# The product with w2 as seven products of quarters instead of eight, in 24 of its 32 row tiles

## The chip, the cores and the metric

The kernel runs on one core of a Trainium2 chip, as one program in one launch. The metric is the device time in microseconds; for a pair of kernels it is measured on the same chip. The kernel before took 1195.74 us, the median of three runs between 1192.88 and 1196.31.

## The reference

The reference is a decoder trunk of two layers on 512 tokens of 1024 columns, all in float32. Each layer is a token mixer and an MLP, and each of the four parts ends in a layer norm:

```python
D_MODEL = 1024; SEQ = 512; DEPTH = 2; D_FF = 4 * D_MODEL
ALPHA = (2 * DEPTH) ** 0.25
x = layer_norm(ALPHA * x + mixer(x), g, b)             # stick-breaking attention and SSM, then sparse attention
x = layer_norm(ALPHA * x + square(relu(x @ w1)) @ w2, g, b)     # w1: 1024 x 4096, w2: 4096 x 1024
```

Only the MLP is changed. Let H stand for the squared relu, 512 tokens by 4096.

## The kernel before

A float32 product is made of three products on TensorE in a format that it reads at one column per cycle. Each operand is split into a high part (a cast to that format, on ScalarE, line 104, tile `whi`) and a low part (the operand less its high part, on VectorE, line 105, tile `wlo`, for some tiles on GpSimd instead). Then high by high, high by low and low by high are added up in one accumulator. The activations are kept transposed, as `xhi` and `xlo`.

The MLP (function `mlp`) goes through the 4096 columns of H in eight groups of 512. For each group it computes four row tiles of H, 128 rows by 512 tokens each: a tile is 24 matmuls of 128x512 (lines 131 to 133; eight slices of the 1024 model columns, three matmuls each) into an accumulator `psa`. ScalarE takes the relu (line 222) and writes its square as the high part (line 224); VectorE squares the relu too (line 223) and subtracts the high part from it (line 225). Then the group's 512 rows of w2 are multiplied in: for each half of the columns and each of four token tiles, 12 matmuls of 128x512 (`mlp_block`, lines 255 to 257) into an accumulator `psb`, which VectorE adds to `x` (line 262). A group thus has 96 matmuls with w1 and 96 with w2. An MLP has 768 and 768.

The first four tiles of each MLP are computed in two halves of the tokens (`proj_halves`), so that they can begin as soon as two token tiles have left the layer norm ahead of it. For each token tile the layer norm (`layer_norm`) is a chain on VectorE: two statistics (line 181), their sum (182), the variance (183), a power on GpSimd (184), two scalings (185, 189), then TensorE transposes the tile (line 199), ScalarE casts the transpose (202) and VectorE subtracts (203). The out projection of the mixer, whose blocks (lines 716 to 718 and the addition to `x` on line 721 or 723) feed the layer norm, runs interleaved with it.

The order of the instructions on each engine is set when the kernel is built, by a scheduler that works from the program's order, the dependences and the free buffers; at run time each engine takes its instructions in that order and waits where an operand is not there. `raw` has three buffers, `whi` and `wlo` four each in each of two pools, `psb` four. Weights are loaded by DMAs that SyncE issues in its own fixed order.

Of the kernel before, what the change touches and what calls it, by code (L numbers as in the profile page):

```python
# [8 lines left out]
F32 = mybir.dt.float32  # L9
F32R = mybir.dt.float32r  # L10
AF = mybir.ActivationFunctionType
ALU = mybir.AluOpType
# [3 lines left out]
P = 128  # L16
S = 512
D = 1024
KT = D // P
NB = S // P  # L20
FF = 4096
ALPHA = 4.0 ** 0.25
# [13 lines left out]
class Trunk:  # L36
# [50 lines left out]
        self.n += 1  # L87
        return f"{s}_{self.n}"

    def w_tiles(self, pool=None):  # L90
        wp = pool or self.wp
        return (wp.tile([P, 1024], F32, tag="raw", bufs=3, name=self.nm("raw")),
                wp.tile([P, 1024], F32R, tag="whi", bufs=4, name=self.nm("whi")),
                wp.tile([P, 1024], F32R, tag="wlo", bufs=4, name=self.nm("wlo")))

    def weights(self, srcs, n=1024, eng=None, pool=None, parts=1):

        nc = self.nc
        raw, hi, lo = self.w_tiles(pool)
# [8 lines left out]
    def w_cols(self, w, c0, eng=None, pool=None):  # L108
# [4 lines left out]
        hi, lo = self.weights(srcs, eng=eng, pool=pool)  # L113
        return hi.rearrange("p (k c) -> p k c", c=P), lo.rearrange("p (k c) -> p k c", c=P)

    def w_rows(self, w, r0, c0, eng=None, pool=None, parts=1):
# [9 lines left out]
        hi, lo = self.weights(srcs, eng=eng, pool=pool, parts=parts)  # L126
        return hi.rearrange("p (k c) -> p k c", c=512), lo.rearrange("p (k c) -> p k c", c=512)

    def mm3(self, ps, lhi, llo, rhi, rlo, start, stop):
# [73 lines left out]
            nc.vector.tensor_tensor(self.xlo[:, 4 * h:4 * h + 4, tok], pv, hi.bitcast(F32), ALU.subtract)  # L203

    def mlp(self, w1, w2, g, b, last):
        nc = self.nc
        if self.n_mlp == 0:
            self.open_psb()
            self.kept = False
        self.n_mlp += 1  # L210
        with self.tc.tile_pool(name=self.nm("mlp"), bufs=2, side="right", reuse_waits="tile") as hp:
            ng = FF // 512
            for grp in range(ng):
                hhi = hp.tile([P, 4, S], F32R, tag="hhi", name=self.nm("hhi"))
                hlo = hp.tile([P, 4, S], F32R, tag="hlo", name=self.nm("hlo"))
                if grp == 0:
                    pss = self.proj_halves([self.w_cols(w1, f * P, nc.gpsimd, hp) for f in range(4)])
# [8 lines left out]
                ws = [[self.w_rows(w2, grp * 512 + i * 256, half * 512, pool=hp if half or grp < ng - 1 else self.wp)  # L226
                       for i in range(2)] for half in range(2)]
                part = lambda half, h=(hhi, hlo), ws=ws: (*h, ws[half])
                if grp < ng - 2:
                    for half in range(2):  # L230
                        for t in range(NB):
                            self.mlp_block([part(half)], t, half, grp == 0)
                elif grp == ng - 2:
                    for t in range(NB):
                        self.mlp_block([part(0)], t, 0, False)
                    held = part(1)
                else:
                    def both(t):
                        self.mlp_block([part(0)], t, 0, False)
                        n = 256 if last and t == NB - 1 else 512  # L240
                        for c0 in range(0, 512, n):
                            self.mlp_block([held, part(1)], t, 1, False, c0, n)
                    self.blocks_and_norms([lambda t=t: both(t) for t in range(NB)], self.ln_params(g, b), last,
                                          2 if last else 1)

    def mlp_block(self, parts, t, half, first, c0=0, n=512):
# [830 lines left out]
```

## Time and profile before

| what | value |
|---|---|
| median of three runs | 1195.74 us |
| the profiled execution | 1195.17 us, of it 1193.4 us in the span |
| TensorE busy | 1141.6 us, 96% of the span |
| VectorE, ScalarE, GpSimd busy | 61%, 37%, 16% |
| granted clock of TensorE, mean | 0.987 of full speed |

A full clock (1.00) is the level of 2.4 GHz, 0.50 the level of 1.2 GHz. The span has four stages: the first mixer until about 265 us, the first MLP until 600, the second mixer until 860, the second MLP from there to the end. Matmuls are pipelined in the profile: each lasts longer than the time to the next one, so the cost of a row of matmuls is read from their starts, and the time that a row lasts tells when its result can be used. The chain that ended last is followed back from the last instruction; what stands in it set the end.

### The profile page before, as it was taken

Reading aid. Unit: us, or ns where it says so; the run is one execution under the profiler, and the core shown is the slowest. Engines: PE = TensorE matmul, PEld = TensorE weight load, DVE = VectorE, ACT = ScalarE, POOL = GpSimd, SP = SyncE. Lnnn points to the kernel's source line nnn. Section 1 sums busy time; section 2 is a strip of 40 time slices with the busy share of each in tenths; the row PEclk is TensorE's granted clock in tenths of the full one; section 3 lists DMA queues with packets and bytes.
Section 4 is the critical chain, followed back from the end, with each engine's and each line's share of the span. In section 5 each row is a group of like instructions: output and inputs, shape, how many; then the busy total and the mean of one; then the engine's idle time right before and its main releaser. Section 6 shows DMA issues by size and latency. Waiting matters only on the chain.

```text
span 1193.4 us, 15777 instructions
## 1 busy us (share of the span) xinstructions
PE 1141.6 (96%) x6004; PEld 952.2 (80%) x6004; DVE 724.5 (61%) x1183; ACT 443.2 (37%) x734; POOL 193.2 (16%) x209
## 2 busy tenths in 40 slices
PE   7989998999999999999999959998999999999997
PEld 6878776798888888888898847777988888888886
DVE  7996598685444444444568997539544444444436
ACT  5534487323322332323145437643322332332320
POOL 1044130450000000000021735327000000000001
PEclk9998999999999999999999979999999999999999
DMA  7536772643332332332155840025422332332201
GB/s 239 141 79 147 196 228 54 177 120 111 106 98 79 106 107 71 106 96 51 36 146 150 216 136 1 2 60 172 140 89 88 106 106 71 106 106 74 69 1 71
DMA packets 147307, 127.00 MB, mean 106 GB/s; under 512 B 24352, under 2 KB 115296, under 8 KB 147232
## 3 DMA queue, kind: packets, MB, share of 16 engines
q1 hardware_dynamic: 145552, 123.59, 36.2%
q10 hardware_dynamic: 1680, 2.41, 0.6%
q8 instruction: 47, 0.77, 0.3%
q14 instruction: 28, 0.23, 0.1%
HBM read 105.80 MB, written 5.37 MB: 93 GB/s over the span
## 4 chain that ended last, share of the span: by engine, by line
PE 82%; DVE 11%; DMA 3%; issue 2%; ACT 1%; SPq 1%; POOLq 0%; DVEq 0%; POOL 0%; ACTq 0%
PE psa L132 11%; PE psa L133 11%; PE psa L131 11%; PE psb L257 10%; PE psb L256 10%; PE psb L255 10%; PE pso L824 3%; PE pst L817 2%; DVE acc L989 2%; DVE top L988 2%; PE psl L1011 2%; PE psb L716 2%; PE psb L718 2%; PE psb L717 2%; DVE sh L498 1%
## 5 line engine op out<-in xcount | busy, mean ns | idle before, releaser
L104 ACT CAST whi<-raw 128x1024 fp32r<-128x1024 f32 (+1 forms) x177 | 184.5, 1048 | 482.3 <-PE psb L257 249.5
L105 DVE TENSOR_TENSOR wlo<-raw,whi 128x1024 fp32r<-128x1024 f32 (+1 forms) x142 | 179.8, 1268 | 194.3 <-ACT whi L104 194.0
L132 PE MATMUL psa<-xlo,whi 128*128 128x512 f32 (+1 forms) x720 | 267.1, 372 | 2.4 <-DVE xlo L203 2.4
L133 PE MATMUL psa<-xhi,wlo 128*128 128x512 f32 (+1 forms) x720 | 267.6, 372 | 0.0
L131 PE MATMUL psa<-xhi,whi 128*128 128x512 f32 (+1 forms) x720 | 265.9, 372 | 0.2 <-ACT xhi L202 0.2
L255 PE MATMUL psb<-whi,hhi 128*128 128x512 f32 (+1 forms) x520 | 200.6, 386 | 0.0
L256 PE MATMUL psb<-wlo,hhi 128*128 128x512 f32 (+1 forms) x520 | 200.5, 386 | 0.0
L257 PE MATMUL psb<-whi,hlo 128*128 128x512 f32 (+1 forms) x520 | 193.0, 386 | 0.0
L262 DVE TENSOR_TENSOR x<-x,psb 128x512 f32<-128x512 f32 (+1 forms) x105 | 69.2, 679 | 148.3 <-PE psb L257 148.2
L132 PEld LDWEIGHTS psa<-xlo,whi 128*128 128x128 f32 x720 | 136.4, 189 | 25.7 <-DVE xlo L203 2.6
L133 PEld LDWEIGHTS psa<-xhi,wlo 128*128 128x128 f32 x720 | 136.3, 189 | 23.0
L131 PEld LDWEIGHTS psa<-xhi,whi 128*128 128x128 f32 x720 | 135.7, 190 | 23.2 <-ACT xhi L202 0.5
L105 POOL TENSOR_TENSOR wlo<-raw,whi 128x1024 fp32r<-128x1024 f32 x35 | 93.6, 2686 | 144.8 <-ACT whi L104 143.7
L257 PEld LDWEIGHTS psb<-whi,hlo 128*128 128x128 f32 x520 | 97.7, 188 | 19.6
L256 PEld LDWEIGHTS psb<-wlo,hhi 128*128 128x128 f32 x520 | 97.7, 188 | 19.6
L255 PEld LDWEIGHTS psb<-whi,hhi 128*128 128x128 f32 x520 | 97.7, 188 | 19.5
L184 POOL TENSOR_TENSOR rs<-rs,two 128x1 f32<-128x1 f32 x16 | 21.1, 1318 | 408.8 <-DVE rs L183 408.7
L716 PE MATMUL psb<-whi,xhi 128*128 128x512 f32 x128 | 50.6, 400 | 2.3 <-DVE x L721 2.3
L717 PE MATMUL psb<-wlo,xhi 128*128 128x512 f32 x128 | 50.1, 392 | 0.8 <-DVE wlo L105 0.8
L718 PE MATMUL psb<-whi,xlo 128*128 128x512 f32 x128 | 50.4, 394 | 0.0
L225 DVE TENSOR_TENSOR hlo<-h,hhi 128x512 fp32r<-128x512 f32 x64 | 44.3, 693 | 6.4
L223 DVE TENSOR_TENSOR h<-r 128x512 f32<-128x512 f32 x64 | 43.8, 685 | 6.5 <-ACT r L222 6.5
(240 smaller groups left out, 1481.6 us busy)
## 6 DMA issues: line engine op xcount, KB each, us to landing
raw<-in_w_dram SPq DMA_DIRECT2D x128, 512.0 KB, 4.1
raw<-in_w_in_dram SPq DMA_DIRECT2D x29, 512.0 KB, 4.3
raw<-in_w_out_dram SPq DMA_DIRECT2D x16, 512.0 KB, 4.5
qst<-hl SPq DMA_DIRECT2D x48, 128.0 KB, 2.9
kst<-hl SPq DMA_DIRECT2D x24, 256.0 KB, 4.4
gb<-in_ln_g_dram SPq DMA_DIRECT2D x4, 512.0 KB, 3.7
gb<-in_ln_b_dram SPq DMA_DIRECT2D x4, 512.0 KB, 5.5
x<-in_x_dram SPq DMA_DIRECT2D x4, 512.0 KB, 6.8
```

Of the source, the lines that this page charges most:

```text
L104: nc.scalar.copy(hi[:, c], raw[:, c])
L105: (eng or nc.vector).tensor_tensor(lo[:, c], raw[:, c], hi[:, c].bitcast(F32), ALU.subtract)
L131: mm(ps, lhi, rhi, start=start, stop=False)
L132: mm(ps, lhi, rlo, start=False, stop=False)
L133: mm(ps, llo, rhi, start=False, stop=stop)
L255: nc.tensor.matmul(ps, lh, whi, start=f + i == 0, stop=False)
L256: nc.tensor.matmul(ps, lh, wlo, start=False, stop=False)
L257: nc.tensor.matmul(ps, ll, whi, start=False, stop=f == 3 and i == len(parts) - 1)
L262: nc.vector.tensor_tensor(xs, xs, ps, ALU.add)
L716: nc.tensor.matmul(ps, chi[:, k, tok], whi, start=i == 0, stop=False)
L717: nc.tensor.matmul(ps, chi[:, k, tok], wlo, start=False, stop=False)
L718: nc.tensor.matmul(ps, clo[:, k, tok], whi, start=False, stop=k == tiles[-1])
```

## The change

In each MLP the first six groups are taken in three chunks of 1024 rows, and the product of H with these rows of w2 is computed by Strassen's method in Winograd's form. The tokens, the 1024 rows and the columns are each cut in two, so that H gives four quarters (`a11`, `a21`: the first 512 rows, for tokens 0 to 255 and 256 to 511; `a12`, `a22`: the other 512 rows) and w2 four (`b11`, `b12`, `b21`, `b22`). Seven products of a combination of quarters with another take the place of eight. A product (lines 311 to 313) is 24 matmuls of 128x512 into two accumulators, so a chunk has 168 matmuls with w2 where two groups had 192. The combinations of quarters of w2 (line 293) and of H (lines 334, 345, 347, 354) and the additions of the accumulators to `x` (lines 320, 323) and to a buffer `u` (line 331) are VectorE's, except that ScalarE writes `u` the first time (line 329). `u` is added to three quarters of `x` at the end of the third chunk (line 367).

The tiles of H of a chunk stay float32: ScalarE takes the relu (line 227) and squares it in place (line 228). High and low parts are made of each combination just before its product (lines 298 and 299). The program writes one product, then one tile of H of the next chunk, and so on; after the seventh product come the last two tiles, and then the next chunk. The last two groups are computed as before (ScalarE now does the square and the cast, lines 237 and 238). GpSimd no longer subtracts for the four tiles after the first four of each MLP; VectorE does.

The other functions of the diff only pass a buffer's name on, so that the new tiles share space. Lines of the new kernel behind this place are 124 higher than before (the out projection's 716 to 723 are 840 to 847).

```diff
     def mlp(self, w1, w2, g, b, last):
...
-                for f in range(4):
-                    ps = pss[f] if grp == 0 else self.proj_fm(w1, grp * 512 + f * P, nc.gpsimd if grp == 1 else None)
-                    r = hp.tile([P, S], F32, tag="r", name=self.nm("r"))
-                    h = hp.tile([P, S], F32, tag="h", name=self.nm("h"))
-                    nc.scalar.activation(r, ps, AF.Relu)
-                    nc.vector.tensor_tensor(h, r, r, ALU.mult)
-                    nc.scalar.activation(hhi[:, f, :], r, AF.Square)
-                    nc.vector.tensor_tensor(hlo[:, f, :], h, hhi[:, f, :].bitcast(F32), ALU.subtract)
...
+            def up_raw(c, first=False):
+                hs = [h_tile(F32) for _ in range(2)]
+                pss = self.proj_halves([self.w_cols(w1, f * P, nc.gpsimd, hp, ("b21", "b22")[f // 2])
+                                        for f in range(4)]) if first else ()
+                for f in range(8):
+                    if f < len(pss):
+                        ps = pss[f]
+                    else:
+                        ps = self.proj_fm(w1, (c * 8 + f) * P, None)
+                    h = hs[f // 4][:, f % 4, :]
+                    nc.scalar.activation(h, ps, AF.Relu)
+                    nc.scalar.activation(h, h, AF.Square)
+                    yield hs
...
+            for hs in up_raw(0, True):
+                pass
+            u = hp.tile([P, 2, 512], F32, tag="u", bufs=1, name=self.nm("u"))
+            touched = set()
+            for c in range(3):
+                ups = up_raw(c + 1) if c < 2 else itertools.chain(up_split(6), up_split(7))
+                got = []
+                for _ in self.down_chunk(hp, w2, c * 1024, hs, u, touched, c == 2):
+                    got += itertools.islice(ups, 1)
+                got += ups
+                hs = got[-1]
...
+    def down_chunk(self, hp, w2, r0, hs, u, touched, last):
+        nc, mm = self.nc, self.nc.tensor.matmul
+        vec, act = nc.vector, nc.scalar
+        a11, a21 = hs[0][:, :, 0:256], hs[0][:, :, 256:512]
+        a12, a22 = hs[1][:, :, 0:256], hs[1][:, :, 256:512]
...
+        def halves(src, pool, c):
...
+            act.copy(hi, src)
+            vec.tensor_tensor(lo, src, hi.bitcast(F32), ALU.subtract)
+            return hi, lo
+
+        def product(a, b):
+            pss = [self.psb.tile([P, 512], F32, tag="psb", name=self.nm("psb")) for _ in range(2)]
+            ahi, alo = halves(a, self.wp, 256)
+            for i in range(2):
+                bhi, blo = halves(b[i], hp, 512)
+                for t, ps in enumerate(pss):
+                    tok = slice(t * P, (t + 1) * P)
+                    for k in range(2):
+                        lh, ll = ahi[:, 2 * i + k, tok], alo[:, 2 * i + k, tok]
+                        mm(ps, lh, bhi[:, k, :], start=i + k == 0, stop=False)
+                        mm(ps, lh, blo[:, k, :], start=False, stop=False)
+                        mm(ps, ll, bhi[:, k, :], start=False, stop=i + k == 2)
+            return pss
...
+        b12, b11 = load("b12", 0, 1), load("b11", 0, 0)
+        vec.tensor_tensor(a21, a21, a22, ALU.add)
+        combine(b12, b12, b11, ALU.subtract)
+        ps = product(a21, b12)
+        add(ps, 1, 1)
+        add(ps, 0, 1)
+        yield
+        b22 = load("b22", 1, 1)
+        ps = product(a11, b11)
+        add(ps, 0, 0)
+        gather(ps)
+        yield
+        vec.tensor_tensor(a11, a21, a11, ALU.subtract)
+        s4 = hp.tile([P, 4, 256], F32, tag="s4", bufs=1, name=self.nm("s4"))
+        vec.tensor_tensor(s4, a12, a11, ALU.subtract)
+        add(product(s4, b22), 0, 1)
+        yield
...
+        add(product(a22, b22), 1, 0, ALU.subtract)
+        if last:
+            for row, col in ((0, 1), (1, 0), (1, 1)):
+                xs = self.x[:, 2 * row:2 * row + 2, col * 512:col * 512 + 512]
+                vec.tensor_tensor(xs, xs, u, ALU.add)
+        yield
```

The scheduler's order is shown at three places. The first is TensorE in the first MLP, where the work with w1 ends and that with w2 begins. Before, behind the last tile of the second group (`psa_506`), stand blocks of its product (`psb_521`, `psb_522`), whose first operands are slices 0 to 2 of H (`hhi_483`):

```order
L132 MATMUL psa_506_2955<-xlo_72,whi_504_2950 128x512
L133 MATMUL psa_506_2955<-xhi_71,wlo_505_2951 128x512
L255 MATMUL psb_521_3010<-whi_510_2987,hhi_483_2836 128x512 [waits DVE_49,Activation_49]
L256 MATMUL psb_521_3010<-wlo_511_2988,hhi_483_2836 128x512
L257 MATMUL psb_521_3010<-whi_510_2987,hlo_484_2837 128x512 [waits DVE_49]
L255 MATMUL psb_521_3010<-whi_510_2987,hhi_483_2836 128x512 [waits Activation_49]
```

Now, at the second chunk, behind the last of its eight tiles (`psa_570`) stands the first product (`psb_575`, `psb_576`), whose `whi_577` is the high part of `a21` plus `a22`:

```order
L132 MATMUL psa_570_3371<-xlo_72,whi_568_3366 128x512
L133 MATMUL psa_570_3371<-xhi_71,wlo_569_3367 128x512
L311 MATMUL psb_575_3409<-whi_579_3415,whi_577_3411 128x512 [waits Activation_49]
L312 MATMUL psb_575_3409<-wlo_580_3416,whi_577_3411 128x512
L311 MATMUL psb_576_3410<-whi_579_3415,whi_577_3411 128x512
L312 MATMUL psb_576_3410<-wlo_580_3416,whi_577_3411 128x512
L131 MATMUL psa_588_3459<-xhi_71,whi_586_3454 128x512 [waits Activation_49]
L132 MATMUL psa_588_3459<-xlo_72,whi_586_3454 128x512
L313 MATMUL psb_575_3409<-whi_579_3415,wlo_578_3412 128x512 [waits DVE_49]
```

The product that needs all eight tiles has moved to the place right behind the last of them. The second place is VectorE in the layer norm ahead of the first MLP. Before (`psb_393` to `psb_399` are blocks of the out projection, 723 is the addition to `x`):

```order
L723 TENSOR_TENSOR x_1307<-x_1307,psb_393_2234 128x512 [waits PE_49]
L181 BN_STATS st_404_2318<-x_1307 128x6 [waits DVE_49]
L723 TENSOR_TENSOR x_1307<-x_1307,psb_395_2248 128x512 [waits PE_49]
L181 BN_STATS st_404_2318<-x_1307 128x6 [waits DVE_49]
L182 BN_AGGR mv_405_2319<-st_404_2318 128x2 [waits DVE_49]
L183 TENSOR_SCALAR rs_406_2320<-mv_405_2319 128x1 [waits DVE_49]
L185 SCALAR_TENSOR_TENSOR x_1307<-x_1307,mv_405_2319,gb_169_1311 128x1024
```

Now the first combination of quarters of w2 (`b12` less `b11`, two tiles) stands among them:

```order
L847 TENSOR_TENSOR x_1307<-x_1307,psb_393_2234 128x512 [waits PE_49]
L181 BN_STATS st_404_2318<-x_1307 128x6 [waits DVE_49]
L847 TENSOR_TENSOR x_1307<-x_1307,psb_395_2248 128x512 [waits PE_49]
L181 BN_STATS st_404_2318<-x_1307 128x6 [waits DVE_49]
L293 TENSOR_TENSOR b12_472_2817<-b12_472_2817,b11_474_2821 128x1024 [waits DMAHW6_49,DMAHW4_49]
L182 BN_AGGR mv_405_2319<-st_404_2318 128x2 [waits DVE_49]
L293 TENSOR_TENSOR b12_473_2819<-b12_473_2819,b11_475_2823 128x1024 [waits DMAHW7_49,DMAHW5_49]
L847 TENSOR_TENSOR x_1307<-x_1307,psb_397_2262 128x512 [waits PE_49]
L183 TENSOR_SCALAR rs_406_2320<-mv_405_2319 128x1 [waits DVE_49]
L185 SCALAR_TENSOR_TENSOR x_1307<-x_1307,mv_405_2319,gb_169_1311 128x1024
```

Two subtractions came between the statistics and the scaling of the first token tile. The third place is TensorE ahead of the second MLP, behind the last block of the out projection (`psb_1279`, token tile 3). Before, the transposes of token tile 1 stand there (`pst_1284`, `pst_1286`), and then the first tiles of H (`psa_1316` to `psa_1319`):

```order
L718 MATMUL psb_1279_7190<-whi_1263_7083,xlo_72 128x512
L199 MATMUL pst_1284_7226<-ident_73,x_1307 128x128 [waits DVE_49]
L199 MATMUL pst_1284_7226<-ident_73,x_1307 128x128 x3
L199 MATMUL pst_1286_7233<-ident_73,x_1307 128x128 [waits PE_49]
L199 MATMUL pst_1286_7233<-ident_73,x_1307 128x128 x3
L131 MATMUL psa_1316_7320<-xhi_71,whi_1305_7297 128x256 [waits Activation_49]
```

Now those of token tile 2 stand there too (`pst_1305`, `pst_1307`):

```order
L842 MATMUL psb_1293_7213<-whi_1277_7106,xlo_72 128x512
L199 MATMUL pst_1298_7249<-ident_73,x_1307 128x128 [waits DVE_49]
L199 MATMUL pst_1298_7249<-ident_73,x_1307 128x128 x3
L199 MATMUL pst_1300_7256<-ident_73,x_1307 128x128 [waits DVE_49]
L199 MATMUL pst_1300_7256<-ident_73,x_1307 128x128 x3
L199 MATMUL pst_1305_7273<-ident_73,x_1307 128x128 [waits DVE_49,PE_49]
L199 MATMUL pst_1305_7273<-ident_73,x_1307 128x128 x3
L131 MATMUL psa_1330_7343<-xhi_71,whi_1319_7320 128x256 [waits Activation_49]
```

The first tile of H now stands behind the layer norm of a third token tile.

## Rows read from the trace of the kernel before

**Rows 1.** Busy time by stage: stretch, length, engines (instructions), clock, DMA share, GB/s.
```profile
265.00:600.00 335.00, 335.00 (x1535) 279.67 (x1534) 161.29 (x203) 100.12 (x129) 4.33 (x4) 1.00 0.30 89
860.00:1193.40 333.40, 325.77 (x1460) 270.53 (x1458) 156.97 (x199) 87.75 (x111) 5.83 (x4) 0.99 0.27 82
```
**Rows 2.** The page, part 5: groups, busy, mean ns, idle before and releaser.
```profile
L132 PE MATMUL psa<-xlo,whi 128*128 128x512 f32 (+1 forms) x720 | 267.1, 372 | 2.4 <-DVE xlo L203 2.4
L257 PE MATMUL psb<-whi,hlo 128*128 128x512 f32 (+1 forms) x520 | 193.0, 386 | 0.0
```
**Rows 3.** Timeline of TensorE in the first MLP: start, us, what.
```profile
320.24 0.39 PE L133 MATMUL psa<-xhi,wlo 128*128 128x512 f32 x1
...
328.17 0.39 PE L256 MATMUL psb<-wlo,hhi 128*128 128x512 f32 x1
```
**Rows 4.** Timelines of ScalarE and VectorE there.
```profile
320.48 1.05 ACT L104 CAST whi<-raw 128x1024 fp32r<-128x1024 f32 x1 [3.23 <-PE psa L132]
321.44 0.59 ACT L222 ACTIVATE r<-psa 128x512 f32<-128x512 f32 x1
322.06 0.63 ACT L224 ACTIVATE hhi<-r 128x512 fp32r<-128x512 f32 x1
...
321.56 1.23 DVE L105 TENSOR_TENSOR wlo<-raw,whi 128x1024 fp32r<-128x1024 f32 x1 [2.82 <-ACT whi L104]
329.05 1.29 DVE L262 TENSOR_TENSOR x<-x,psb 128x512 f32<-128x512 f32 x2 [4.86 <-PE psb L257]
```
**Rows 5.** Timeline of VectorE in the layer norm ahead of the first MLP.
```profile
235.70 2.42 DVE L185 SCALAR_TENSOR_TENSOR x<-x,mv,gb 128x1024 f32<-128x1024 f32 x1
...
242.18 1.27 DVE L185 SCALAR_TENSOR_TENSOR x<-x,mv,gb 128x1024 f32<-128x1024 f32 x1
243.37 0.68 DVE L723 TENSOR_TENSOR x<-x,psb 128x512 f32<-128x512 f32 x1
243.97 1.28 DVE L189 SCALAR_TENSOR_TENSOR x<-x,rs,gb 128x1024 f32<-128x1024 f32 x1
```
**Rows 6.** Timelines of GpSimd and TensorE there.
```profile
225.60 11.44 POOL L105 TENSOR_TENSOR wlo<-raw,whi 128x1024 fp32r<-128x1024 f32 x4 [21.72 <-ACT whi L104]
...
241.90 1.03 PE L199 MATMUL pst<-ident,x 128*128 128x128 f32 x8
245.53 0.60 PE L199 MATMUL pst<-ident,x 128*128 128x128 f32 x4
245.91 0.49 PE L716 MATMUL psb<-whi,xhi 128*128 128x512 f32 x1
```
**Rows 7.** Timeline of VectorE in the layer norm ahead of the second MLP.
```profile
811.26 2.22 DVE L105 TENSOR_TENSOR wlo<-raw,whi 128x1024 fp32r<-128x1024 f32 x1
828.41 3.32 DVE L185 SCALAR_TENSOR_TENSOR x<-x,mv,gb 128x1024 f32<-128x1024 f32 x1
```
**Rows 8.** Timeline of TensorE there, and at an earlier wait.
```profile
821.33 1.03 PE L199 MATMUL pst<-ident,x 128*128 128x128 f32 x8
829.81 0.74 PE L131 MATMUL psa<-xhi,whi 128*128 128x256 f32 x4 [0.24 <-ACT xhi L202]
832.98 0.38 PE L132 MATMUL psa<-xlo,whi 128*128 128x256 f32 x1 [2.43 <-DVE xlo L203]
...
229.84 0.47 PE L716 MATMUL psb<-whi,xhi 128*128 128x512 f32 x1 [2.05 <-DVE x L721]
```
**Rows 9.** Busy time and granted clock (third number from the end) around three waits.
```profile
230.00:231.00 1.00, 1.00 (x5) 0.82 (x5) 1.00 (x1) 0.00 (x0) 1.00 (x1) 1.00 1.02 303
834.00:835.00 1.00, 1.00 (x6) 1.00 (x6) 0.93 (x4) 0.00 (x0) 1.00 (x2) 0.50 0.04 10
836.00:837.00 1.00, 1.00 (x7) 1.00 (x6) 1.00 (x1) 0.00 (x0) 1.00 (x2) 0.50 1.09 329
714.00:715.00 1.00, 0.54 (x2) 0.54 (x3) 1.00 (x5) 0.56 (x2) 0.00 (x0) 0.50 0.00 0
716.00:717.00 1.00, 1.00 (x5) 0.91 (x4) 1.00 (x5) 0.99 (x5) 0.00 (x0) 0.50 0.00 0
```

More of the change, by code (lines that the diff above doesn't have):

```diff
@@ L88, in nm, with w_tiles, weights @@
         return f"{s}_{self.n}"
-    def w_tiles(self, pool=None):
+    def w_tiles(self, pool=None, tag=None):
         wp = pool or self.wp
-        return (wp.tile([P, 1024], F32, tag="raw", bufs=3, name=self.nm("raw")),
+        return (wp.tile([P, 1024], F32, tag=tag or "raw", bufs=2 if tag else 3, name=self.nm("raw")),
                 wp.tile([P, 1024], F32R, tag="whi", bufs=4, name=self.nm("whi")),
                 wp.tile([P, 1024], F32R, tag="wlo", bufs=4, name=self.nm("wlo")))
-    def weights(self, srcs, n=1024, eng=None, pool=None, parts=1):
+    def weights(self, srcs, n=1024, eng=None, pool=None, parts=1, tag=None):
         nc = self.nc
-        raw, hi, lo = self.w_tiles(pool)
+        raw, hi, lo = self.w_tiles(pool, tag)
         for view, src in srcs(raw):
@@ L106, in weights, with w_cols @@
         return hi, lo
-    def w_cols(self, w, c0, eng=None, pool=None):
+    def w_cols(self, w, c0, eng=None, pool=None, tag=None):
         def srcs(raw):
@@ L112, in srcs, with w_rows @@
                    w[:, c0:c0 + P].rearrange("(k p) c -> p k c", p=P))
-        hi, lo = self.weights(srcs, eng=eng, pool=pool)
+        hi, lo = self.weights(srcs, eng=eng, pool=pool, tag=tag)
         return hi.rearrange("p (k c) -> p k c", c=P), lo.rearrange("p (k c) -> p k c", c=P)
-    def w_rows(self, w, r0, c0, eng=None, pool=None, parts=1):
+    def w_rows(self, w, r0, c0, eng=None, pool=None, parts=1, tag=None):
         def srcs(raw):
@@ L125, in srcs @@
                     yield rv[:, k, :], wv[:, k, :]
[L126 removed]
+        hi, lo = self.weights(srcs, eng=eng, pool=pool, parts=parts, tag=tag)
         return hi.rearrange("p (k c) -> p k c", c=512), lo.rearrange("p (k c) -> p k c", c=512)
@@ new lines, in mlp @@
+            h_tile = lambda dt: hp.tile([P, 4, S], dt, tag="h", bufs=4, name=self.nm("h"))
+            def up_raw(c, first=False):
[11 more added lines that the diff above has]
+                    yield hs
@@ new lines, in up_split @@
+            def up_split(grp):
+                hhi, hlo = h_tile(F32R), h_tile(F32R)
+                for f in range(4):
+                    ps = self.proj_fm(w1, grp * 512 + f * P, None)
+                    h = hp.tile([P, S], F32, tag="r", bufs=1, name=self.nm("r"))
+                    nc.scalar.activation(h, ps, AF.Relu)
+                    nc.scalar.activation(h, h, AF.Square)
+                    nc.scalar.copy(hhi[:, f, :], h)
+                    nc.vector.tensor_tensor(hlo[:, f, :], h, hhi[:, f, :].bitcast(F32), ALU.subtract)
+                    yield hhi, hlo
@@ new lines, in mlp @@
+            ng = 8
+            for grp, h in ((6, got[3]), (7, got[7])):
+                ws = [[self.w_rows(w2, grp * 512 + i * 256, half * 512, pool=hp if half or grp < ng - 1 else self.wp,
+                                   tag=(("b12", "b11")[half] if grp < ng - 1 else "b21") if half or grp < ng - 1
+                                   else None)
+                       for i in range(2)] for half in range(2)]
+                part = lambda half, h=h, ws=ws: (*h, ws[half])
+                if grp == ng - 2:
@@ L244, in mlp, with load, combine, add @@
                                           2 if last else 1)
+    def down_chunk(self, hp, w2, r0, hs, u, touched, last):
[3 more added lines that the diff above has]
+        a12, a22 = hs[1][:, :, 0:256], hs[1][:, :, 256:512]
+        def load(tag, j, n):
+            ts = []
+            for i in range(2):
+                t = hp.tile([P, 1024], F32, tag=tag, bufs=2, name=self.nm(tag)).rearrange("p (k c) -> p k c", c=512)
+                r = r0 + j * 512 + i * 256
+                nc.sync.dma_start(t, w2[r:r + 256, n * 512:n * 512 + 512].rearrange("(k p) c -> p k c", p=P))
+                ts.append(t)
+            return ts
+        def combine(out, x, y, op):
+            for o, p, q in zip(out, x, y):
+                vec.tensor_tensor(o, p, q, op)
+        def halves(src, pool, c):
+            hi = pool.tile([P, 1024], F32R, tag="whi", bufs=4, name=self.nm("whi")).rearrange("p (k c) -> p k c", c=c)
+            lo = pool.tile([P, 1024], F32R, tag="wlo", bufs=4, name=self.nm("wlo")).rearrange("p (k c) -> p k c", c=c)
+            act.copy(hi, src)
[4 more added lines that the diff above has]
+            ahi, alo = halves(a, self.wp, 256)
+            for i in range(2):
+                bhi, blo = halves(b[i], hp, 512)
[7 more added lines that the diff above has]
+            return pss
+        def add(pss, row, col, op=ALU.add):
+            for t, ps in enumerate(pss):
+                xs = self.x[:, 2 * row + t, col * 512:col * 512 + 512]
+                if (row, col, t) in touched:
+                    vec.tensor_tensor(xs, xs, ps, op)
+                else:
+                    touched.add((row, col, t))
+                    vec.scalar_tensor_tensor(xs, xs, ALPHA, ps, ALU.mult, op)
+        def gather(pss):
+            for t, ps in enumerate(pss):
+                if ("u", t) not in touched:
+                    touched.add(("u", t))
+                    act.copy(u[:, t, :], ps)
+                else:
+                    vec.tensor_tensor(u[:, t, :], u[:, t, :], ps, ALU.add)
+        b12, b11 = load("b12", 0, 1), load("b11", 0, 0)
[15 more added lines that the diff above has]
+        yield
+        combine(b12, b22, b12, ALU.subtract)
+        b21 = load("b21", 1, 0)
+        gather(product(a11, b12))
+        yield
+        vec.tensor_tensor(a11, a22, a11, ALU.subtract)
+        combine(b11, b12, b11, ALU.subtract)
+        ps = product(a11, b11)
+        add(ps, 1, 0)
+        add(ps, 1, 1)
+        yield
+        combine(b22, b12, b21, ALU.subtract)
+        add(product(a12, b21), 0, 0)
+        yield
+        add(product(a22, b22), 1, 0, ALU.subtract)
[3 more added lines that the diff above has]
+                vec.tensor_tensor(xs, xs, u, ALU.add)
+        yield
```

13 lines of the change are left out of this document (removed).

## The prediction

> **What bounds the kernel now.** I first read the busy time by stage [rows 1]. In the first MLP TensorE is busy for 335.00 of 335.00 us at a granted clock of 1.00, VectorE for 161.29, ScalarE for 100.12 and GpSimd for 4.33; the second MLP is nearly the same. The reader is to see an engine without a gap beside three with half their time or more to spare. The page's groups [rows 2] say the same by line: the matmuls with w2 (line 257) have no idle time before them, and those with w1 (line 132) had to wait 2.4 us in the whole run. So in the MLPs nothing but the number of matmuls sets the time. The timeline [rows 3] gives the price of one: from 320.24 to 328.17 are 35 matmuls, 0.2266 us each, though a row lasts 0.39. The last views are the timelines of VectorE, ScalarE and TensorE where the MLPs begin [rows 5 to 8], since there, and only there, TensorE hangs on VectorE.
>
> I make the sum against the profiled execution, 1195.2 us (1193.4 in the span); it lies 0.6 below the median of the three runs.
>
> **The matmuls removed.** A chunk has 168 matmuls with w2 in place of 192, of the same shape. There are three chunks in each of two MLPs, so 6 x 24 = 144 go, at 0.2266 us [rows 3]: -32.6 us. In the MLPs TensorE is never idle, so all of it lies on the path.
>
> **The stop at the head of each chunk.** The first product of a chunk takes `a21` plus `a22`, and these reach over all eight tiles of H. On TensorE it stands right behind the eighth tile, and TensorE takes its instructions in order, so nothing can fill the time in between. It waits for: the end of the tile's last matmul, 0.39 after its start [rows 3] and 0.03 to hand over (the cast of 320.48 ends at 321.53, and VectorE's subtraction starts at 321.56 [rows 4]); the relu, whose square follows 0.62 after it; the square, 0.63 [rows 4]; the sum on VectorE, 128x1024 from two operands in SBUF, which the trace doesn't show at this line, but line 189 is of that size and kind and took 1.28 [rows 5]; the cast, 1.05 [rows 4]; and three more hand-overs, 0.09. Together 0.42 + 0.62 + 0.63 + 1.28 + 1.05 + 0.09 = 4.09 us after the last matmul's start, of which the next matmul's slot was 0.23: a stop of 3.86 us. Its bounds: not under 3.0, even if the sum should cost as little as two 128x512 pieces that follow each other without a gap (0.60 each, [rows 5]) and the hand-overs nothing; 5.4 if the sum took the 2.42 to 3.32 that such pieces took beside GpSimd [rows 5 to 7], but GpSimd is quiet in the MLPs [rows 1]. I take 3.86, and six times that is +23.2 us. Behind the waiting product stand the rest of it and the next tile of H, so the whole of TensorE's queue is late. Before, a group's first block needed its last slice only at the end, and these waits were covered.
>
> **Inside a chunk.** TensorE has 15 x 24 matmuls, 81.6 us. VectorE has 41 pieces of 128x1024 (21 subtractions for the products, 8 for w1, 8 combinations of w2, 4 of H) and 20 additions of 128x512. From start to start the first cost 1.19 and the second 0.60 [rows 5], 61 us together. ScalarE has 29 casts at 1.05 and 8 pairs at 1.25, some 40 us. Followed product by product, each operand of the second to seventh product is ready 7 us or more ahead of TensorE, since a tile of H (5.4 us) lies between two products. I cost all this at nothing; the cover is the 5.4 us of a tile, and if the slack of 20 us on VectorE went, each product would wait for its own operand.
>
> **The clock.** Before, TensorE stopped twice for over 2 us near the MLPs. After the stop that ended at 832.98 (2.43 us) the granted clock fell to 0.50, the level of 1.2 GHz, within a microsecond and was back at 837 [rows 8, 9]. After the one that ended at 229.84 (2.05 us) it stayed at 1.00 [rows 8, 9]. A long stop that ended in the slice of 714 left it at 0.50 until 717 [rows 9]. So a stop of 3.9 us lies beyond the one that cost something. About 3 us at half the clock lose half of that: 1.7 us by the first row, 1.3 by the last. I take 1.4 for each stop, with bounds of 0 and 1.7. Six at the chunks and one at the first MLP's layer norm (below) make +9.8 us. The Trainium skill's page "TensorE: Matmul & The Clock Gate", section "Why this matters for your kernels", says that an idle gap between bursts of matmuls can send the clock back to half, which speaks against this change. By that rule all seven stops cost; the trace agrees in two of its three stops. By the stop at 229.84 none would.
>
> **The first MLP's start.** VectorE does the layer norm here, and two combinations (line 293) now stand between the statistics and the scaling of token tile 0. From 235.4 they and the sum of the statistics take 2.34 (beside GpSimd, which subtracts until 237.04 [rows 6]; line 185 took 2.42 there [rows 5]), 0.24 and 1.19; then an addition 0.60, the variance 0.07 and the scaling 1.19: 241.0, where before it was 238.0. From there to the end of token tile 1 are three statistics, three additions, two scalings by the power, one by the mean, and two small ones: 6 x 0.60 + 3 x 1.19 + 0.40 = 7.6, so 248.6. TensorE, which now does the last block of token tile 2 first (12 matmuls from 241.90 [rows 6]) and the first transposes after it, is there at 245.4. It stops for 3.2 us and begins the next block at 249.4 with all transposes done, where before it began at 245.91 with 0.4 of them to do: +3.1. Ahead of the second half of the tokens only four matmuls now cover cast and subtraction, where there were eleven: +0.8. Together +3.9, with bounds of 0 (all the combinations in time that VectorE waits anyway) and 6.
>
> **The second MLP's start.** The combinations stand ahead of the last subtraction for the out projection (at 811.26 before [rows 7]); this is hidden, since TensorE has other token tiles to do until 818. But the three token tiles now end together, at 818.8, 820 and 821, and not one by one. From 819.3 VectorE has three additions, four statistics, two sums of them, the variance and two scalings up to the end of token tile 0: 7 x 0.60 + 0.55 + 1.19 + 1.28 = 7.2, so 826.5. TensorE needs it at 821.33 [rows 8]. Behind it follow 7.0 us for token tiles 1 and 2, three subtractions for w1 that GpSimd did before (3 x 1.15), an addition and the subtraction for token tile 1 (0.60 each): 838.2, where TensorE went on at 832.98 [rows 8]. That is +5.2. The fall of the clock behind the first of these two stops is hidden by the second, and the one behind the second was there before. VectorE gains there too: GpSimd no longer stretches a scaling to 3.32 us [rows 7], and that is in these numbers. Bounds: -2.4 (the wait of before gone) and +8 (a weight tile of the out projection, now loaded behind eight others, late by 3).
>
> **The end of each MLP.** Three additions of `u` (1.19 each) and ScalarE's extra pass go beside 34 us of matmuls, of which VectorE needs some 27: 0, bounds -2 and +2.
>
> **The sum.** 1195.2 - 32.6 + 23.2 + 9.8 + 3.9 + 5.2 = 1204.7 us.
>
> **The rivals.** First, the clock holds through stops of 3.9 us, as it did at 229.84: 1204.7 - 9.8 = 1194.9, no change. For it speaks one row, against it two. Second, on the other side: at both MLP starts the quiet GpSimd pays more than the added pieces cost. Line 185 and the like took 2.42 to 3.32 beside it and 1.27 alone [rows 5, 7]; if VectorE got through both layer norms before TensorE needed them, the 9.1 us of the starts would not come, nor the clock's 1.4 there, and the old wait of 2.43 with its fall of 1.7 would go: 1204.7 - 9.1 - 1.4 - 4.1 = 1190.1, faster. It decides at the scaling of token tile 1, which would have to end before 245.4. Against it stands the order, in which the combinations are ahead of that scaling. The page "SBUF — State Buffer", section "Who interferes with whom", of the Trainium skill says that a VectorE instruction with two inputs in SBUF contends with a GpSimd instruction that reads it; the rows of line 185 agree, and by that rule the whole stretch goes away with GpSimd's work. Third, VectorE becomes the bound inside the chunks: at the 2.42 us of a disturbed piece, 41 of them and 20 x 0.60 would need 111 us against 85.5, 26 more in each chunk and some 1350 in all; a tenth of that, from a queue in which single pieces come late, gives 1220. Against it: GpSimd is quiet there.
>
> **Chances and range.** The forecast 0.66, with a range of its own of 1199 to 1211 from the bounds of the clock and the two starts; the clock holds 0.18; the quiet GpSimd 0.09; VectorE late 0.07. A measurement of this kernel can tell about 0.3% (3.6 us) from no change. So faster 0.11 (the second rival and the low end of the first), same 0.20 (the rest of the first and the forecast's lowest part), slower 0.69. From 1191 to 1212 holds 8 in 10.
>
> **What would show it.** Right: six waits of 3.5 to 4.2 us of line 311 for ScalarE's line 298, a granted clock of 0.50 for about 3 us behind each, 144 rows fewer on TensorE, and waits of the transposes (line 199) for VectorE at both MLP starts. Wrong: stops under 3 us, a clock of 1.00 behind them, or waits of line 311 or 312 in the middle of a chunk, which would mean that a product's operands come late and that the time is longer than forecast.

## The result and the profile after

The changed kernel takes 1204.73 us, the median of eight runs between 1198.71 and 1206.58. The kernel before took 1195.30 in the runs beside them. The ratio is 1.0075 with a 95% interval of 1.0057 to 1.0093: slower, by less than 1%. The forecast was 1204.7. How well it came out step by step is another matter: the sections below show that the term for the clock was too small and those for the starts of the MLPs too large, by about as much.

The profiled execution took 1203.52 us, 1201.7 of it in the span. Busy time by stage, as in [rows 1], of the changed kernel:

```profile
265.00:600.00 335.00, 323.71 (x1449) 268.37 (x1447) 215.03 (x227) 143.79 (x176) 3.43 (x3) 0.97 0.27 80
860.00:1201.70 341.70, 323.07 (x1442) 267.70 (x1440) 219.47 (x238) 138.21 (x167) 5.82 (x4) 0.97 0.25 76
```

Against [rows 1], TensorE now has gaps in the first MLP (323.71 of 335.00) and its mean clock is 0.97 in place of 1.00. VectorE is at two thirds of the time, not at its limit. Who TensorE waited for, in the whole run (total, times, longest; the list's lines on the mixers and two of 0.2 us are left out):

```profile
PE psb L311 <- ACT whi L298: 22.1, 6, 3.7
...
PE pst L199 <- DVE rs L183: 4.8, 1, 4.8
...
PE pst L199 <- DVE x L189: 2.0, 1, 2.0
...
PE pst L199 <- DVE x L845: 0.7, 1, 0.7
PE psb L840 <- DVE rs L183: 0.6, 1, 0.6
```

The first line is new: line 311 waits six times, 3.7 us each, once at the head of each chunk. The others are the two layer norms. There is no line for the inside of a chunk. One stop in detail, at the second chunk (timelines of TensorE, ScalarE and VectorE of the changed kernel):

```profile
387.38 0.39 PE L133 MATMUL psa<-xhi,wlo 128*128 128x512 f32 x1
391.45 0.80 PE L311 MATMUL psb<-whi,whi 128*128 128x512 f32 x1 [3.68 <-ACT whi L298]
...
387.81 0.60 ACT L227 ACTIVATE h<-psa 128x512 f32<-128x512 f32 x1 [4.18 <-PE psa L133]
388.44 0.63 ACT L228 ACTIVATE h<-h 128x512 f32<-128x512 f32 x1
390.36 1.04 ACT L298 CAST whi<-h 128x1024 fp32r<-128x1024 f32 x1 [1.29 <-DVE h L334]
...
389.10 1.22 DVE L334 TENSOR_TENSOR h<-h,h 128x1024 f32<-128x1024 f32 x1 [7.85 <-ACT h L228]
```

Relu, square, sum and cast follow one another from 387.81 to 391.40, and VectorE and ScalarE had nothing else in between. The two matmuls are 4.07 us apart, 3.84 more than a matmul's slot. Behind the stop the matmuls of this product start 0.43 us apart, where the price at full clock was 0.2266 [rows 3]. The granted clock (third number from the end) of the changed kernel, behind the first stop of the first MLP and the first of the second:

```profile
301.00:302.00 1.00, 0.00 (x0) 0.00 (x0) 1.00 (x1) 0.00 (x0) 0.00 (x0) 0.99 0.00 0
303.00:304.00 1.00, 0.72 (x2) 0.63 (x3) 0.74 (x1) 1.00 (x2) 0.00 (x0) 0.50 0.00 0
307.00:308.00 1.00, 1.00 (x4) 0.81 (x3) 1.00 (x2) 0.00 (x0) 0.00 (x0) 0.50 0.76 221
309.00:310.00 1.00, 1.00 (x6) 0.82 (x5) 0.97 (x2) 0.66 (x1) 0.00 (x0) 1.00 0.60 167
...
891.00:892.00 1.00, 0.58 (x3) 0.48 (x3) 0.60 (x1) 1.00 (x2) 0.00 (x0) 1.00 0.00 0
893.00:894.00 1.00, 1.00 (x4) 0.81 (x3) 1.00 (x2) 1.00 (x2) 0.00 (x0) 0.50 0.00 0
896.00:897.00 1.00, 1.00 (x6) 0.82 (x5) 1.00 (x2) 0.45 (x1) 0.00 (x0) 1.00 1.07 323
```

The first fall lasts from 302 to past 308, the second from past 892 to 895. All six stops are followed by a fall; three are of the long kind. Counted over the matmuls behind each stop, a fall of the short kind cost 1.5 to 1.7 us and one of the long kind 2.7 to 3.0.

To see where the time went, I cut the span of each profiled execution at four places that can be found in every trace: the last matmul of the first four tiles of each MLP (the last 128x256 one there), and the first 128x256 matmul behind the rest of each MLP. Lengths in us:

| kernel | until MLP 1 is under way | rest of MLP 1 | mixer 2 and start of MLP 2 | rest of MLP 2 | end |
|---|---|---|---|---|---|
| before | 276.80 | 328.35 | 253.60 | 321.10 | 13.5 |
| changed | 277.52 | 330.82 | 257.32 | 322.56 | 13.5 |
| second product first | 278.82 | 312.04 | 256.50 | 304.78 | 13.5 |
| stop filled | 277.85 | 324.14 | 257.96 | 316.88 | 13.5 |
| stop half filled | 281.25 | 325.71 | 255.87 | 316.99 | 13.5 |
| GpSimd at the starts | 279.69 | 330.90 | 259.00 | 322.74 | 13.5 |
| second first, GpSimd | 278.90 | 312.04 | 257.17 | 304.79 | 13.5 |
| late loads alone | 278.85 | 330.84 | 253.56 | 321.09 | 13.5 |
| second first, late loads | 273.79 | 312.04 | 252.04 | 304.78 | 13.5 |

The rests of the MLPs, which lost 72 matmuls each, became 2.5 and 1.5 us longer.

### The profile page after: what moved, and what is told of

It is laid out like the page before. It is cut to its first block, busy times and chain, and to the rows that moved or that the text cites. A ratio compares the mean times of both kernels' runs of the same rounds, so it can differ in the third digit from the quotient of the medians.

```text
span 1201.7 us, 15563 instructions
## 1 busy us (share of the span) xinstructions
PE 1125.3 (94%) x5860; PEld 934.5 (78%) x5860; DVE 842.7 (70%) x1255; ACT 533.6 (44%) x832; POOL 173.1 (14%) x201
## 4 chain that ended last, share of the span: by engine, by line
PE 77%; DVE 13%; DMA 4%; ACT 3%; issue 2%; SPq 1%; POOL 0%; POOLq 0%; DVEq 0%; ACTq 0%
PE psa L132 11%; PE psa L131 11%; PE psa L133 11%; PE psb L311 7%; PE psb L312 7%; PE psb L313 7%; PE pso L948 3%; PE psb L379 2%; PE psb L381 2%; PE psb L380 2%; PE pst L941 2%; DVE acc L1113 2%; DVE top L1112 2%; PE psb L840 2%; PE psb L842 1%
## 5 line engine op out<-in xcount | busy, mean ns | idle before, releaser
L105 DVE TENSOR_TENSOR wlo<-raw,whi 128x1024 fp32r<-128x1024 f32 (+1 forms) x102 | 127.9, 1258 | 79.0 <-ACT whi L104 78.6
L311 PE MATMUL psb<-whi,whi 128*128 128x512 f32 x336 | 136.0, 405 | 22.1 <-ACT whi L298 22.1
L133 PEld LDWEIGHTS psa<-xhi,wlo 128*128 128x128 f32 x720 | 135.7, 188 | 23.1
L299 DVE TENSOR_TENSOR wlo<-b,whi 128x1024 fp32r<-128x1024 f32 x84 | 102.6, 1222 | 52.2 <-ACT whi L298 52.0
L312 PE MATMUL psb<-wlo,whi 128*128 128x512 f32 x336 | 134.8, 401 | 0.0
L313 PE MATMUL psb<-whi,wlo 128*128 128x512 f32 x336 | 133.1, 399 | 0.0
L298 ACT CAST whi<-b 128x1024 fp32r<-128x1024 f32 x84 | 88.4, 1052 | 55.8 <-PE psb L313 43.9
L311 PEld LDWEIGHTS psb<-whi,whi 128*128 128x128 f32 x336 | 66.0, 196 | 38.5 <-ACT whi L298 24.6
L313 PEld LDWEIGHTS psb<-whi,wlo 128*128 128x128 f32 x336 | 65.5, 195 | 14.3
L312 PEld LDWEIGHTS psb<-wlo,whi 128*128 128x128 f32 x336 | 65.7, 195 | 13.7
L293 DVE TENSOR_TENSOR b<-b,b 128x1024 f32<-128x1024 f32 x48 | 63.2, 1317 | 11.2 <-DMA b<-in_w_dram 10.3
```

Source lines behind the costliest of these rows:

```text
L133: mm(ps, llo, rhi, start=False, stop=stop)
L293: vec.tensor_tensor(o, p, q, op)
L298: act.copy(hi, src)
L299: vec.tensor_tensor(lo, src, hi.bitcast(F32), ALU.subtract)
L311: mm(ps, lh, bhi[:, k, :], start=i + k == 0, stop=False)
L312: mm(ps, lh, blo[:, k, :], start=False, stop=False)
```

## The experiments

The theory was that the stops and the clock behind them eat the gain, and that the starts of the MLPs cost a little more. Its rival was that a chunk is bound by VectorE or by its buffers, and the stop only shows it.

**The second product first.** It needs `a11` and `b11` alone, so the chunk's first four tiles:

```diff
-        b12, b11 = load("b12", 0, 1), load("b11", 0, 0)
-        vec.tensor_tensor(a21, a21, a22, ALU.add)
-        combine(b12, b12, b11, ALU.subtract)
-        ps = product(a21, b12)
...
-        b22 = load("b22", 1, 1)
+        b11 = load("b11", 0, 0)
         ps = product(a11, b11)
         add(ps, 0, 0)
         gather(ps)
         yield
+        b12 = load("b12", 0, 1)
+        vec.tensor_tensor(a21, a21, a22, ALU.add)
+        combine(b12, b12, b11, ALU.subtract)
+        ps = product(a21, b12)
```

> The second product of each chunk (a11 by b11), which needs the chunk's first four tiles only, is put ahead of the first. Theory: the six stops at the heads of the chunks (3.85 us each from start to start) and the half clock behind them (7.3 us in the first MLP and 6.5 in the second, by the gaps between matmuls in the trace of the changed kernel) are the whole reason why the change doesn't pay. Then both go: 1204.7 - 23.1 - 13.8 = 1167.8 us. Rival: the chunk is bound by VectorE or by the buffers of the operands, and the stop only shows it: the wait moves to the product that now comes second, and the time stays above 1195.

Measured: 1167.23 us, ratio 0.9762 (0.9744 to 0.9780). The two MLPs in this kernel, by stretch:

```profile
265.00:590.00 325.00, 324.76 (x1494) 270.98 (x1493) 222.11 (x238) 146.68 (x179) 4.90 (x4) 1.00 0.28 85
850.00:1152.00 302.00, 302.00 (x1334) 250.08 (x1333) 205.85 (x220) 131.46 (x157) 3.30 (x3) 1.00 0.27 82
```

TensorE is busy for all but 0.24 us, at a clock of 1.00, and nothing moved to the product that now comes second. The rests of the MLPs are 312.04 and 304.78: 16.3 us below before in each, and 72 matmuls at 0.2266 are 16.3. The work inside a chunk costs nothing, and the rival is out. The medians differ by 37.5 us from the changed kernel; 36.6 of it are in the two rests (330.82 and 322.56 before this edit), and they are stops and clock together.

**The stop filled.** This tells the two apart: matmuls of no use, whose results the product overwrites, run where TensorE would stand still.

```diff
                 bhi, blo = halves(b[i], hp, 512)
+                for d in range(0 if i else fill):
+                    mm(pss[d % 2], bhi[:, 0, 0:P], bhi[:, 1, :], start=True, stop=True)
...
-        ps = product(a21, b12)
+        ps = product(a21, b12, 17)
```

> Order of products as in the changed kernel, but ahead of each first product stand 17 extra matmuls of 128x512 on operands that are there, 3.85 us, into accumulators that the product then overwrites. They don't let it begin earlier; they keep TensorE at work. Theory: the stops stay as lost time, the falls of the clock behind them go: 1204.7 - 13.8 = 1190.9 us, at a granted clock of 1.00 in the MLPs. Rival: the slow matmuls behind a stop are slow for their operands and not for the clock: 1204.7 or more. By the prediction's 1.4 us a stop it would be 1196.3.

Measured: 1192.06 us, ratio 0.9969 (0.9957 to 0.9981). The head of the second chunk, and the granted clock behind it:

```profile
385.16 0.39 PE L133 MATMUL psa<-xhi,wlo 128*128 128x512 f32 x1
385.39 4.01 PE L308 MATMUL psb<-whi 128*128 128x512 f32 x17
389.25 0.50 PE L313 MATMUL psb<-whi,whi 128*128 128x512 f32 x1
389.59 0.39 PE L314 MATMUL psb<-wlo,whi 128*128 128x512 f32 x1
```

```profile
391.00:392.00 1.00, 1.00 (x6) 0.82 (x5) 1.00 (x2) 1.00 (x2) 0.00 (x0) 1.00 0.00 0
393.00:394.00 1.00, 1.00 (x6) 0.81 (x6) 1.00 (x2) 0.85 (x1) 0.00 (x0) 1.00 0.75 200
```

The product begins 4.09 us behind the start of the tile's last matmul, for 4.07 in the changed kernel, but at a clock of 1.00. So the lost slots cost 12.1 us in each MLP (324.14 less 312.04), and the clock the rest: 330.82 less 324.14 are 6.7 in the first and 322.56 less 316.88 are 5.7 in the second, 12.4 in all. With matmuls that compute nothing the kernel is 0.3% faster than before; without them 0.75% slower.

**The stop half filled**, with 8 such matmuls in place of 17.

> As the run with the filled stop, but with 8 extra matmuls in place of 17: 1.8 us of work and 2.0 us without, six times. Before the change a stop of 2.05 us was followed by a clock of 1.00 and one of 2.43 by a fall. Theory: the rest of 2.0 us costs no clock, and the time is that of the filled stop, 1192 us. Rival: what counts is any gap of this size, the clock falls as behind the whole stop, and the time is 1199 to 1205.

Measured: 1191.46 us, ratio 0.9976 (0.9965 to 0.9987), the same as filled. In its profile line 313 (the product's first matmul) waits as often as before, for half as long, and of six such waits only the first of the first MLP was followed by a fall:

```profile
PE psb L313 <- ACT whi L298: 11.2, 6, 1.9
```

```profile
309.00:310.00 1.00, 1.00 (x4) 0.77 (x3) 1.00 (x2) 0.80 (x1) 0.00 (x0) 0.50 0.00 0
...
395.00:396.00 1.00, 1.00 (x6) 0.72 (x5) 1.00 (x2) 1.00 (x3) 0.00 (x0) 1.00 0.00 0
480.00:481.00 1.00, 1.00 (x5) 0.72 (x6) 1.00 (x2) 1.00 (x2) 0.00 (x0) 1.00 0.00 0
```

A stop of 1.9 us costs the clock one time in six here, one of 3.7 us six times in six, and as often in each of the two other runs that kept the six stops (GpSimd at the starts, late loads alone). One in six is no price for such a stop at other places, though. The same wait of 2.0 us for line 189 ahead of the first MLP stands in four traces; the clock held behind it in that of the changed kernel and fell in those of the second product first, the filled and the half filled stop. Here the changed kernel and the second product first:

```profile
247.00:248.00 1.00, 1.00 (x6) 0.83 (x5) 1.00 (x2) 0.52 (x2) 0.00 (x0) 1.00 0.00 0
247.00:248.00 1.00, 1.00 (x4) 0.81 (x3) 1.00 (x3) 0.23 (x1) 0.00 (x0) 0.50 0.00 0
```

So whether the clock falls behind a stop of 2 us is not settled by its length, and no run here tells what else does it.

**GpSimd at the starts.** The other question was the layer norms ahead of the MLPs.

```diff
-                        ps = self.proj_fm(w1, (c * 8 + f) * P, None)
+                        ps = self.proj_fm(w1, (c * 8 + f) * P, nc.gpsimd if first else None)
...
-        combine(b12, b12, b11, ALU.subtract)
+        combine(b12, b12, b11, ALU.subtract, vec if r0 else nc.gpsimd)
```

> As the changed kernel, but in each MLP GpSimd makes the first chunk's first combination of w2 (two pieces) and the low parts of tiles five to eight of w1, as before the change. Theory: at the second MLP these pieces on VectorE delay its layer norm, so that the wait of 4.8 us for the first transposes gets shorter: 2 to 3 us in all, 1202 us. Rival: GpSimd's work stretches VectorE's scalings as before (2.4 to 3.4 us in place of 1.3), and what one gains the other loses: 1205 us or more.

Measured: 1203.47 us, ratio 1.0070 (1.0051 to 1.0088); the interval holds the changed kernel's 1.0075, so no effect is shown. The waits ahead of the first MLP got longer and the one ahead of the second stayed, though VectorE had six pieces less in this part of each MLP:

```profile
PE pst L199 <- DVE x L189: 4.3, 2, 3.2
...
PE pst L199 <- DVE rs L183: 4.9, 1, 4.9
```

**Both edits.**

> The second product first, and GpSimd for the pieces at the MLPs' starts: the first and third edit together. Theory: the two are independent, 1167.8 less 2 to 3 us, 1165.3. Rival: with the stops gone the delays at the starts are hidden differently and the second edit gives nothing: 1168 or more.

Measured: 1168.38 us, ratio 0.9768 (0.9746 to 0.9790), no better than the first edit alone; the wait ahead of the second MLP was 4.9 us in both. So VectorE's added pieces are not what the start of the second MLP waits for.

**Late loads.** What stays is the order of TensorE, in which the out projection's token tiles end together. Its last weight tile is loaded behind eight other loads there. A copy of one column makes the loads of the first chunk wait for the first normalised token tile; in the order of TensorE the token tiles end one by one again.

```diff
+                if r0 == 0:
+                    vec.tensor_copy(t[:, 0, 0:1], self.x[:, 0, 0:1])
                 nc.sync.dma_start(t, w2[r:r + 256, n * 512:n * 512 + 512].rearrange("(k p) c -> p k c", p=P))
```

> As the run with the second product first, and in the first chunk of each MLP a one-column copy from the first normalised token tile into each tile of w2 ahead of its load, so that these loads (and the combinations behind them) can't go ahead of the out projection's last weight tile and into the layer norm. In the order of TensorE the out projection's token tiles then end one by one again. Theory: the waits of 4.9 us ahead of the second MLP and of 2.0 ahead of the first, with the clock's falls behind them, come from these loads and combinations alone: 1167.2 less 4 to 7, 1161.5 us. Rival: the layer norm on VectorE takes as long in any order, and its wait only moves to the next transposes: 1167 us.

Measured, with the second product first: 1158.38 us, ratio 0.9699 (0.9686 to 0.9712), 8.9 us less than without the late loads, or 7.5 by the two ratios, more than expected. By the table 5.0 us came at the first start and 4.5 in the column of the second. At the first start TensorE waits for neither line 183 nor line 189 any more; the waits that are left stand at the second:

```profile
PE psa L132 <- DVE xlo L203: 1.8, 1, 1.8
...
PE pst L199 <- DVE x L189: 0.8, 1, 0.8
```

> As the changed kernel, with the late loads of the run above alone: the first product stays first, and the six stops with it. Theory: 4 to 7 us less than the changed kernel's 1204.7, 1199 us, so that the starts of the MLPs, which the prediction had at 9.1 us, are worth no more than that. Rival: nothing is gained, 1204.7.

Measured, with the first product first: 1199.78 us, ratio 1.0043 (1.0029 to 1.0058), about 5 us less than the changed kernel, or 3.8 by the ratios, as expected. The table has the gain in the column of the second start (257.32 to 253.56), where the wait of 4.8 us became one of 0.8 and one of 2.0; at the first start nothing was gained in this run (277.52 to 278.85), where a wait of 2.7 us for line 203, with a fall of the clock behind it, took the place of the others. The column has the second mixer in it, so I cut it once more, at the longest wait in that mixer (before, changed kernel, this run):

```profile
714.47 4.01 PE L1011 MATMUL psl<-kst,qst 128*128 128x384 f32 x16 [14.62 <-DVE pst L1018]
718.89 3.93 PE L1135 MATMUL psl<-kst,qst 128*128 128x384 f32 x16 [14.63 <-DVE pst L1142]
718.63 4.63 PE L1137 MATMUL psl<-kst,qst 128*128 128x384 f32 x16 [14.61 <-DVE pst L1144]
```

From there to the end of the column it is 144.28 us before, 146.77 in the changed kernel and 144.62 here: all but 0.3 of the 2.5 that the second MLP's start cost. The other 1.6 us lie ahead of this wait, where the edit changes nothing; the next section comes back to them.

The version with the second product first and the late loads is the fastest: 1158.38 against 1194.41 for the kernel before in the runs beside it. Both edits change the order of the work and not what is computed.

## Why the prediction was right, and where it was not

The sign, the place and the time were right. By the table and the experiments, in us:

| step | predicted | measured | from |
|---|---|---|---|
| matmuls removed | -32.6 | -32.6 | second product first, two columns |
| six stops | +23.2 | +23.1 | 6 x 3.85 in the trace |
| clock behind them | +8.4 | +13.4 | rests of the MLPs, less the two above |
| start of MLP 1, with its clock | +5.3 | +0.7 | table |
| mixer 2 and start of MLP 2 | +5.2 | +3.7 | table |
| sum | +9.5 | +8.3 | |

**The matmuls and the stops** came out to a tenth. (The filled stop divides the 36.5 us of stops and clock otherwise, 24.2 to 12.4.) The sum on VectorE, which no row of before showed, took 1.22 where line 189's 1.28 [rows 5] was taken for it. So the chain of four pieces was worth its working: each duration had a row, and since nothing else stood in the queues, the sum of the rows was the wait. Inside a chunk nothing waited, as costed.

**The clock** fell behind every stop, as forecast, but 1.4 us each was too little: 2.4 in the first MLP and 2.1 in the second. That term was mis-sized. It took the fall from the stop that ended at 832.98 [rows 8, 9], which was of the short kind; half of the new ones lasted 6 to 7 us. A fall of the long kind stood in the trace of before, behind a stop of 2.80 us in the first mixer, and so did a stop of 3.09 us without one; the working, which looked near the MLPs and at one wait of the second mixer, has neither:

```profile
77.68 1.06 PE L463 MATMUL psv<-ident,v 128*128 128x128 f32 x8 [3.09 <-DVE v L434]
94.76 0.41 PE L521 MATMUL py<-state,zo 128*128 128x64 f32 x2 [2.80 <-DMA state<-sk]
...
78.00:79.00 1.00, 1.00 (x9) 0.96 (x8) 1.00 (x3) 0.00 (x0) 0.00 (x0) 1.00 0.00 0
97.00:98.00 1.00, 1.00 (x6) 1.00 (x7) 1.00 (x1) 0.00 (x0) 1.00 (x1) 0.50 0.61 198
102.00:103.00 1.00, 1.00 (x6) 1.00 (x5) 1.00 (x2) 0.90 (x2) 0.00 (x0) 0.50 0.00 0
```

The rule of the Trainium skill's page "TensorE: Matmul & The Clock Gate", section "Why this matters for your kernels", that an idle gap can send the clock back to half, agrees with these traces: six of six at 3.7 us, none where the gap was filled.

**The start of MLP 1** was costed at +3.9 and its clock at +1.4; it cost 0.7. The wait for token tile 1 came (2.0 us for 3.2 forecast), but a wait of before went away that the sum had left in, the one of 2.05 us at 229.84 [rows 8]. ScalarE and VectorE there, in the trace before:

```profile
224.47 4.84 ACT L104 CAST whi<-raw 128x1024 fp32r<-128x1024 f32 x5 [4.43 <-DMA raw<-in_w_dram]
...
226.51 2.58 DVE L105 TENSOR_TENSOR wlo<-raw,whi 128x1024 fp32r<-128x1024 f32 x1 [3.43 <-ACT whi L104]
```

And ScalarE, VectorE and GpSimd in the trace after:

```profile
220.59 1.05 ACT L104 CAST whi<-raw 128x1024 fp32r<-128x1024 f32 x1 [0.36 <-DMA raw<-in_w_dram]
223.93 4.98 ACT L104 CAST whi<-raw 128x1024 fp32r<-128x1024 f32 x5 [2.29 <-PE psb L842]
...
225.02 1.23 DVE L105 TENSOR_TENSOR wlo<-raw,whi 128x1024 fp32r<-128x1024 f32 x1 [1.76 <-ACT whi L104]
...
237.08 1.27 DVE L185 SCALAR_TENSOR_TENSOR x<-x,mv,gb 128x1024 f32<-128x1024 f32 x1
...
226.01 8.19 POOL L105 TENSOR_TENSOR wlo<-raw,whi 128x1024 fp32r<-128x1024 f32 x3 [1.89 <-ACT whi L104]
```

Before, ScalarE's row of five casts began at 224.47, when a load of w1 had come, and VectorE's subtraction at 226.51, beside GpSimd, took 2.58. Now the first cast of w1 is done at 221.6, the next row begins when TensorE lets a buffer go, and the subtraction comes 1.5 us earlier and takes 1.23. GpSimd's last three subtractions end at 234.20 and not at 237.04 [rows 6], so the scaling of line 185 has nothing beside it and takes 1.27 where it took 2.42 [rows 5]. I had followed the added pieces and not the loads that the new buffers of the first four tiles let begin sooner. That the earlier cast is the reason is read from these rows; no run undid it alone. The 1.4 us for the clock didn't come because it held behind the wait of 2.0 us in this trace, and that was luck: where it fell behind the same wait, in the three traces named above, the first four tiles were done some 33.4 us after that wait's end and not 31.8.

**The start of MLP 2.** Its first wait was 4.8 us, where the working has some 5.2 (826.5 less 821.33), in the right place and for the reason given first: three token tiles that end together. The second wait was 0.7, where the working had left the old one of 2.43 [rows 8] about as it was, and the clock fell behind the first one alone; +2.5 in place of +5.2. Another 1.2 us came ahead of that, in the mixer: from the end of the MLP's rest to the wait of 14.6 us it is 110.55 us for 109.31. There TensorE stopped for 1.86 us, before for 0.63, and behind it the clock fell, as it didn't before:

```profile
629.46 0.81 PE L1077 MATMUL psx<-kist,qist 96*128 96x256 f32 x3 [1.86 <-issue]
...
630.00:631.00 1.00, 1.00 (x6) 0.78 (x5) 0.48 (x1) 0.88 (x4) 0.00 (x0) 0.50 1.16 322
632.00:633.00 1.00, 1.00 (x6) 1.00 (x6) 0.96 (x3) 0.00 (x0) 0.00 (x0) 0.50 1.08 334
```

In the four other runs of new kernels without a fall there this part takes 108.0 to 109.1 us, in the three with one 109.7 to 110.9. So the 1.2 us go with the fall; why this wait was longer is open. The bound of "a weight tile late" was the right place to look, but the tile was not late: its load was issued at 807.83, where before it was at 803.47, 88.9 and 89.0 us behind the wait of 14.6 us. VectorE's additions that end the three token tiles begin at 823.83, 825.16 and 826.47, before at 815.63, 819.20 and 821.59, and with the late loads alone at 821.62, 823.21 and 829.51. So it is the order of TensorE that made the wait of 4.8 us, and the late loads took it away. They undo the loads' place, the combinations and the order together; that the scheduler derives the order from the time at which it expects the load is the likely reason and wasn't tested alone.

So the figure of 1204.7 is closer than its terms: 5.0 too little for the clock, 6.1 too much for the starts. That these nearly cancel is luck. Of the rivals, the held clock and VectorE as the bound are refuted by the filled stop and by the second product first. An undisturbed VectorE did pay at the first start in part, as the second rival had it, though there GpSimd's subtractions came earlier and were no fewer; the run that gave GpSimd more work gained nothing. Two slips in the working change no term: TensorE waits for VectorE in the mixers too, for 14.6 us at 714.47, and 26 us in each of six chunks on top of 1204.7 are some 1360 and not 1350.

## What to carry to other kernels

A saving in matmuls is worth what it leaves of an unbroken stream: look at which product stands behind the last producer of its operands, add up the chain of small pieces between them from their rows, and add the clock behind each stop. Order the products so that the first of a group needs what was made early; that one edit turned +0.75% into -2.4%. Where loads are put ahead of others, read the order of the engine that uses them, since a scheduler that expects a tile late may rearrange work whose transfer would have been in time.

## What the runs showed of the hardware

The granted clock fell to 0.50, the level of 1.2 GHz, behind all six stops of 3.7 us without a matmul in each of the three kernels that had them, behind one of six of 1.9 us at the same places, and behind none that was filled with matmuls whose results nobody reads. Behind shorter stops it differed from execution to execution: the wait of 2.0 us ahead of the first MLP was followed by a fall in three traces of four. A fall cost 1.5 to 1.7 us of work where it lasted for some 3 us behind the stop, and 2.7 to 3.0 where it lasted for some 6, as from 302 to past 308. The eight runs of the changed kernel differ by 7.9 us; the three kernels without stops in the MLPs had four runs each, which differ by 0.4, 2.1 and 2.5.
